# Packed first loads, early squares and pinned conversions in a two-layer decoder step

## The chip, the core and the metric

The kernel runs on one core of one Trainium2 chip. The metric is the device time of one launch in microseconds, the median of several runs. The profile is of one execution; its rows count from the start of the span.

## The reference

Two layers of a decoder are run for a prompt of 256 rows and eight single-row samples (together T = 264 columns) with shared weights, all in float32. Cut to the part around the change:

```python
def moba_gmlp_mixer(x, pos, past_kv, norm_g, w_in, sgu_gain, sgu_w, sgu_b, w_out):
    h = rmsnorm(x, norm_g)
    z = h @ w_in                                  # 1024 -> q, k, v, bu, bv of 512 each
    q, k = rope_partial(q), rope_partial(k)
    a = moba_attention(q, k_all, v_all, pos)      # prompt: causal softmax; samples: 256 paged rows and their own
    bvn = layer_norm(gelu(bv), sgu_gain)
    b_out = spatial_gating(gelu(bu), bvn, sgu_w, sgu_b)
    return x + concat([a, b_out]) @ w_out
```

A convolutional feed-forward network follows, then a second layer (stick-breaking attention, pooling), another such network and a last RMSNorm. All projections, k and v of both layers and some states are outputs.

## The kernel before, in words

X is held transposed, 128 features by 264 columns in eight slices, the weights as 1472 blocks of 128x128 in the order of use. To keep float32 accuracy every operand is split in a high part of type fp32r and the rest: a block costs three matmuls (lines 329 high by high, 330 weight high by operand rest, 331 weight rest by operand high) that add up in a PSUM bank. The high part of eight blocks (a "tile", `wh`) is made by an ACT copy of 128x1024 (line 306), the rest (`wl`) by a DVE subtraction (line 307); `split` looks three tiles ahead, and there are four buffers of each. Raw weights come in chunks, the first six of 8 blocks (512 KB), then of 16 (1 MB), into a ring of three buffers (`rawp`), by DMAs that SP issues. The text numbers chunks (raw0 to raw5 hold blocks 0 to 47, raw6 holds 48 to 63, raw7 64 to 79), tiles (wh0, wh1, ..., eight blocks each) and blocks (0 to 159 are layer 0's input projection, 160 to 223 its output projection).

The order of instructions on an engine is the list scheduler's, except where `tc.keep_in_program_order` pins one. `run` walks through the blocks and calls hooks: `hk.at(n, f)` calls f after 8(n+1) blocks. Engines take their instructions strictly in that order.

**Opening.** Four loads of X on ACT's queue (lines 343 to 345), raw0 in three pieces, raw1 and raw2 on SP (346 to 351). Eight matmuls of 512 columns on a constant (355 to 357) run before the first operand is there. The first 32 blocks are the four q outputs: for the first five slices of X in turn all four outputs, then the rest output by output (`q0`). For each slice `operand_tile` makes the high part on ACT (373) and the rest on DVE (374), and `Norm.add` squares it on ACT (386) and adds on POOL (395, 398). Two matmuls (406) sum over the partitions; Ln and Exp (408, 409) make R, the reciprocal norm; `rope` is R times cosines and sines on DVE (609 to 611). `in0_evac` takes a finished output from PSUM: for q and k a shuffle (635), two multiplications (637 or 639 on DVE, 640 on POOL) and an addition (641). There are four PSUM banks for projections (`psm`) and four for everything else (`at`). SP reads the sixteen page numbers of the samples into registers (424), each when its first page is loaded; K and V pages are loaded in drips of two.

**Attention and gate.** `s_qk` starts a score bank with a matmul of the mask (658), two heads at a time; ACT makes the exponentials and the normalisation (671 to 675), PE the transposes (684). `masks` converts constants to bf16 on DVE (618 to 624). The gate: gelu of bv at hook GM = 12 (759), the sum for the mean on DVE and that for the variance on POOL (751 to 753), `gm_norm`, transposes, four small matmuls (786), an addition on DVE (787), a multiplication on POOL (790), and `halves` (413, 414) for the operand `catB` with which the output projection begins.

Of the kernel before, what the change touches and what calls it, by code (L numbers as in the profile page):

```python
# [9 lines left out]
F32 = mybir.dt.float32  # L10
# [8 lines left out]
P = 128  # L19
# [18 lines left out]
KQ = 5  # L38
PINM = 8
SQL = 2  # L40
XD = (1, 2, 4, 8)
WARM = 8
YD = ((0, 1), (1, 3), (3, 5), (5, 7), (7, 8))
# [3 lines left out]
GG = 16  # L47
GM = 12
GV = 13.5
# [10 lines left out]
MSK = 4.5  # L60
KL = 0
VL = 9
# [60 lines left out]
def _pack_weights(w_in0, w_out0, w_in1, w_out1, gate, up, down):  # L123
# [28 lines left out]
    return np.concatenate(out)  # L152

# [17 lines left out]
def _consts():  # L171
# [36 lines left out]
_INS = [  # L208
    ("w", (_NB * P * P,)), ("x", (P, KD + KD * T)), ("vec", (P, _NVEC)), ("cst", _CST_ARR.shape), ("rope", (P, 2 * T)),
    ("kt0", (NPHYS, P, 512)), ("vp0", (NPHYS, P, 512)), ("kt1", (NPHYS, P, 512)), ("vp1", (NPHYS, P, 512)),  # L210
# [11 lines left out]
def tile_decoder_step(ctx: ExitStack, tc: tile.TileContext, a):  # L222
# [23 lines left out]

    XG = con.tile([P, KD + KD * T], F32, name="XG")
    GAIN = XG[:, :KD]
    X = XG[:, KD:].rearrange("p (m t) -> p m t", t=T)
    VEC = con.tile([P, _NVEC], F32, name="VEC")  # L250
# [22 lines left out]
    raws, splits = {}, {}  # L273

    def raw(ci):
        if ci not in raws:
            n = _CHUNKS[ci] * P
            r = rawp.tile([P, n], F32, tag="raw", name=f"raw{ci}")
            o = coff[ci] * P * P
            src = a["w"][o:o + P * n].rearrange("(p f) -> p f", p=P)  # L280
            raws[ci] = r
            if ci == 0:
                return lambda c, e: nc.sync.dma_start(r[:, c * P:e * P], src[:, c * P:e * P])
            nc.sync.dma_start(r, src)
        return raws[ci]
# [4 lines left out]
    def split(t):  # L290
        for tt in range(len(splits), min(t + (LOOK if pos[0] else 0), NT - 1) + 1):
# [5 lines left out]
            h = wsp.tile([P, 8 * P], F32R, tag="wh", name=f"wh{tt}")  # L297
            l = wsp.tile([P, 8 * P], F32R, tag="wl", name=f"wl{tt}")
            splits[tt] = (h, l)
            if tt == 0:  # L300
                def piece(c, e, h=h, l=l, src=src):
                    c, e = c * P, e * P
                    tc.keep_in_program_order(v.tensor_copy(h[:, c:e], src[:, c:e]))
                    tc.keep_in_program_order(v.tensor_tensor(l[:, c:e], src[:, c:e], h[:, c:e].bitcast(F32), ALU.subtract))
                return piece
            s.activation(h, src, AF.Copy)  # L306
            v.tensor_tensor(l, src, h.bitcast(F32), ALU.subtract)  # L307
        return splits[t]

    def run(order, rhs, evac, hooks=None):  # L310
        hooks = sorted((hooks or {}).items())
        n = 0
        seen, left, ps = {}, {}, {}
        for m, k in order:
            left[m] = left.get(m, 0) + 1
        for m, k in order:
            i = pos[0]
            pos[0] += 1
            h, l = split(i // 8)
            c = (i % 8) * P  # L320
            if m not in ps:
                ps[m] = psm.tile([P, 512], F32, tag="mm", name=f"mm{i}")
# [6 lines left out]
            pe.matmul(o, h[:, c:c + P], xh, start=first, stop=False)  # L329
            pe.matmul(o, h[:, c:c + P], xl, start=False, stop=False)  # L330
            pe.matmul(o, l[:, c:c + P], xh, start=False, stop=left[m] == 0)  # L331
# [7 lines left out]
    orders = dict(_PHASES)  # L339


    CS = f4("ropecs", (P, 2, T))
    xcut = [0] + [KD + e * T for e in XD]
    for b, e in zip(xcut, xcut[1:]):
        nc.scalar.dma_start(XG[:, b:e], a["x"][:, b:e])
    part = raw(0)
    part(0, 2)
    part(2, 4)
    part(4, 8)
    raw(1)  # L350
    raw(2)
    s.preload_act_table_set("natural_log_exp_and_others")
    warm = con.tile([P, 512], BF16, name="warm")
    v.memset(warm, 1.0)
    pw = at("warm")
    for i in range(WARM):
        tc.keep_in_program_order(pe.matmul(pw, warm[:, :P], warm, start=i == 0, stop=i == WARM - 1))

    def late(dst, src):
        tc.keep_in_program_order(nc.sync.dma_start(dst, src))  # L360

# [17 lines left out]
    class Norm:  # L379
# [3 lines left out]

        def add(self, m, pin=False):
            q = sm.tile([P, T], F32, tag="sq", name=f"sq_{self.name}{m}")
            i = s.activation(q, X[:, m, :], AF.Square)
            if pin:
                tc.keep_in_program_order(i)
# [10 lines left out]

        def finish(self):  # L400
            return rstd_of([self.acc] + self.last, 1.0 / D, self.name)

    def rstd_of(parts, scale, name):
        p = at(f"ns_{name}")
        for i, x in enumerate(parts):
            pe.matmul(p[:, :T], ones, x, start=i == 0, stop=i == len(parts) - 1)
        R = sm.tile([P, T], F32, tag="R", name=f"R_{name}", bufs=2)
# [7 lines left out]

    regs = []

    def page_list(cache, name):
# [3 lines left out]
        def load(i):  # L422
            if len(regs) <= i:
                regs.append(nc.sync.value_load(PT[0:1, i:i + 1], min_val=0, max_val=NPHYS - 1))
            if i % NPG == 0:
# [162 lines left out]
    nrm = Norm("n0", True)  # L588
    piece = split(0)
    pieces = [(0, 2), (2, 4), (4, 8)]  # L590
    for m in range(KD):
        if pieces:
            piece(*pieces.pop(0))
        operand_tile(xg[m // 4], m, X[:, m, :], GAIN[:, m:m + 1], pin=m < PINM)
        if m >= SQL:
            nrm.add(m - SQL, pin=m < PINM)
    for m in range(KD - SQL, KD):
        nrm.add(m)
    raw(3)
    late(CS, a["rope"].rearrange("p (c t) -> p c t", c=2))  # L600
    split(1)
    raw(4)
    late(VEC, a["vec"])
    late(PT, a["pt"])
    late(CST, a["cst"])
    R = nrm.finish()

    rope = f4("rope")
    v.tensor_tensor(rope[:, 0, :], CS[:, 0, :], R, ALU.mult)
    v.scalar_tensor_tensor(rope[:, 2, :], CS[:, 1, :], SCALE, R, ALU.mult, ALU.mult)  # L610
    v.tensor_tensor(rope[:, 1, :], CS[:, 1, :], R, ALU.mult)

# [4 lines left out]
    def masks():  # L617
        tc.keep_in_program_order(v.tensor_copy(maskb0[:, 0:P], cst("m0")))
        v.tensor_copy(maskb0[:, SEQ:384], cst("m0"))
        v.tensor_copy(maskb1[:, 0:P], cst("m1"))  # L620
        v.tensor_copy(maskb1[:, SEQ:384], cst("m1"))
        for mk in (maskb0, maskb1):
            g.memset(mk[:, P:SEQ], 0.0)
        v.tensor_copy(identb, ident)

# [4 lines left out]
    def in0_evac(m, o):  # L630
        n, t = m
        if n in "qk":
            d = (q4 if n == "q" else k4)[:, t, :]
# [8 lines left out]
        else:  # L642
            v.tensor_tensor({"v": v4, "bv": bv4, "bu": bu4}[n][:, t, :], o, R, ALU.mult)

# [96 lines left out]
    def sgu_load():  # L741
        late(sguc[:, 0], a["sguw"].rearrange("p (g t) -> p g t", t=P))
        late(sguc[:, 1], a["sgub"].rearrange("p (g t) -> p g t", t=P))
        tril = sm.tile([P, P], F32, tag="tril", name="tril", bufs=1)
        v.tensor_scalar(tril, cst("m0"), 0.0, None, ALU.is_lt)
        v.tensor_tensor(tril, tril, ident, ALU.add)
# [120 lines left out]
    negU = con.tile([P, P], F32R, name="negU")  # L867
    v.tensor_copy(negU, cst("negU"))
    nonesr = con.tile([P, P], F32R, name="nonesr")
# [156 lines left out]
def _lay(inp):  # L1026
# [6 lines left out]
            "cw": col(f["ffn_conv_w"].reshape(-1)), "cb": col(f["ffn_conv_b"].reshape(-1)),  # L1033
            "w00": np.tile(f["l0_sgu_w"][:, 0, 0][None, :], (P, 1)), "b00": np.tile(f["l0_sgu_b"][:, 0][None, :], (P, 1))}
    return {
        "w": _pack_weights(f["l0_w_in"], f["l0_w_out"], f["l1_w_in"], f["l1_w_out"], f["ffn_w_gate"], f["ffn_w_up"], f["ffn_w_down"]),
        "x": np.concatenate([col(f["l0_norm"]), x.T.reshape(KD, P, T).transpose(1, 0, 2).reshape(P, KD * T)], 1),
        "vec": np.concatenate([vecs[n] for n in _VEC], 1),
# [50 lines left out]
```

## Time and profile before

| what | value |
|---|---|
| time, median of 3 runs | 618.89 us (617.85 to 619.99) |
| the profiled execution's own time | 618.47 us |
| its span | 616.4 us |
| mean granted TensorE clock | 0.996 |
| PE busy | 599.4 us, 4924 matmuls |
| moved by DMA | 121.40 MB, mean 197 GB/s |

The profiled execution takes 2.07 us more than its span. A PE row lasts longer than the distance to the next one, since matmuls overlap, so gaps are read from starts. In a row of the chain or the timeline the first number is the start, the second the duration. A row with SPq or ACTq is an issue of that engine's queue and not the transfer.

### The profile page before, as it was taken

The page shows a single profiled execution, that of the slowest core. Times are in us where ns is not written, and L with a number is a line of the kernel's source. Part 1 is how long each engine was busy: PE and PEld are TensorE (multiplying, and loading weights), DVE is VectorE, ACT ScalarE, POOL GpSimd, SP SyncE. Part 2 cuts the span into 40 slices and gives each one's busy share as a digit, 9 for nine tenths or more (in the row PEclk, how much of TensorE's full clock was granted, in tenths as well). Part 3 has the DMA queues.
Part 4 walks back from the last instruction along what each step waited for, and adds up shares of the span by engine and source line. Part 5 has one row for each costly group of instructions (what it writes and reads, how often), then busy time and mean ns, then how long its engine had stood idle before and what let it go on. Part 6 is the DMA issues. An engine that isn't in the chain of part 4 may idle for free.

```text
span 616.4 us, 12351 instructions
## 1 busy us (share of the span) xinstructions
PE 599.4 (97%) x4924; PEld 575.3 (93%) x4924; DVE 413.1 (67%) x704; ACT 350.4 (57%) x621; POOL 84.9 (14%) x111
## 2 busy tenths in 40 slices
PE   7899999999999999999999999999999999999994
PEld 5788987999999999999999997899999999999994
DVE  6986663969976676655555686396996766764441
ACT  5459763767756555644442757376765555554441
POOL 3330132324200000001110000042420000001020
PEclk9999999999999999999999999999999999999998
DMA  7995873543655445695477559944364555554502
GB/s 259 325 403 220 328 258 54 206 153 133 216 184 205 158 184 205 228 392 200 155 229 262 219 184 141 134 175 172 136 215 170 200 182 167 199 189 166 200 1 70
DMA packets 41354, 121.40 MB, mean 197 GB/s; under 512 B 17490, under 2 KB 19410, under 8 KB 29906
## 3 DMA queue, kind: packets, MB, share of 16 engines
q1 hardware_dynamic: 40178, 119.00, 59.3%
q10 hardware_dynamic: 1120, 1.63, 0.9%
q8 instruction: 38, 0.62, 0.4%
q14 instruction: 18, 0.15, 0.1%
HBM read 116.67 MB, written 3.94 MB: 196 GB/s over the span
## 4 chain that ended last, share of the span: by engine, by line
PE 84%; DVE 7%; issue 3%; DMA 2%; ACT 2%; POOL 1%; SPq 0%; DVEq 0%; ACTq 0%
PE mm L330 26%; PE mm L329 25%; PE mm L331 25%; DMA raw<-in_w 2%; DVE wl L307 2%; DVE xn_l L374 1%; PE pv_l L465 1%; PE sc L451 1%; PE pav L494 1%; PE Z L900 1%; DVE wk L542 1%; ACT wh L306 1%; PE Z L884 1%; POOL wk L553 0%; PE pt L684 0%
## 5 line engine op out<-in xcount | busy, mean ns | idle before, releaser
L307 DVE TENSOR_TENSOR wl<-raw,wh 128x1024 fp32r<-128x1024 f32 x183 | 229.4, 1255 | 129.1 <-ACT wh L306 129.0
L306 ACT ACTIVATE wh<-raw 128x1024 fp32r<-128x1024 f32 x183 | 193.7, 1059 | 182.5 <-PE mm L330 169.3
L330 PE MATMUL mm<-xn_l,wh 128*128 128x264 f32 x544 | 154.7, 284 | 1.7 <-DVE xn_l L374 1.5
L329 PE MATMUL mm<-xn_h,wh 128*128 128x264 f32 x544 | 153.8, 283 | 0.0
L331 PE MATMUL mm<-xn_h,wl 128*128 128x264 f32 x544 | 153.4, 283 | 0.0
L330 PEld LDWEIGHTS mm<-xn_l,wh 128*128 128x128 f32 x544 | 102.3, 188 | 2.5 <-DVE xn_l L374 2.5
L329 PEld LDWEIGHTS mm<-xn_h,wh 128*128 128x128 f32 x544 | 102.1, 188 | 0.0
L331 PEld LDWEIGHTS mm<-xn_h,wl 128*128 128x128 f32 x544 | 102.1, 188 | 0.0
L330 PE MATMUL mm<-a_l,wh 128*128 128x264 f32 x352 | 99.8, 284 | 0.0
L329 PE MATMUL mm<-a_h,wh 128*128 128x264 f32 x352 | 99.5, 284 | 0.0
L331 PE MATMUL mm<-a_h,wl 128*128 128x264 f32 x352 | 99.4, 283 | 0.0
L331 PEld LDWEIGHTS mm<-a_h,wl 128*128 128x128 f32 x352 | 66.2, 188 | 0.0
L330 PEld LDWEIGHTS mm<-a_l,wh 128*128 128x128 f32 x352 | 66.2, 188 | 0.0
L329 PEld LDWEIGHTS mm<-a_h,wh 128*128 128x128 f32 x352 | 66.0, 188 | 0.0
L329 PE MATMUL mm<-xg_h,wh 128*128 128x264 f32 x160 | 46.6, 298 | 3.6 <-DVE q L637 1.6
L330 PE MATMUL mm<-xg_l,wh 128*128 128x264 f32 x160 | 46.1, 293 | 0.0
L331 PE MATMUL mm<-xg_h,wl 128*128 128x264 f32 x160 | 44.7, 291 | 1.3 <-DVE wl L307 1.3
L329 PE MATMUL mm<-xg_f_h,wh 128*128 128x264 f32 x160 | 45.8, 286 | 0.0
L330 PE MATMUL mm<-xg_f_l,wh 128*128 128x264 f32 x160 | 45.4, 284 | 0.0
L331 PE MATMUL mm<-xg_f_h,wl 128*128 128x264 f32 x160 | 45.3, 283 | 0.0
L329 PE MATMUL mm<-xg_n_h,wh 128*128 128x264 f32 x128 | 37.4, 292 | 0.0
L331 PE MATMUL mm<-xg_n_h,wl 128*128 128x264 f32 x128 | 36.8, 288 | 0.0
(266 smaller groups left out, 1074.5 us busy)
## 6 DMA issues: line engine op xcount, KB each, us to landing
raw<-in_w SPq DMA_DIRECT2D x89, 1024.0 KB, 4.8
K<-in_kt SPq DMA_DIRECT2D x32, 256.0 KB, 6.0
V<-in_vp SPq DMA_DIRECT2D x32, 256.0 KB, 5.6
raw<-in_w SPq DMA_DIRECT2D x5, 512.0 KB, 5.3
CST<-in_cst SPq DMA_DIRECT2D x1, 548.0 KB, 5.5
XG<-in_x ACTq DMA_DIRECT2D x1, 528.0 KB, 7.8
out_k<-k SPq DMA_DIRECT2D x1, 528.0 KB, 9.4
out_v<-v SPq DMA_DIRECT2D x1, 528.0 KB, 3.0
```

Source lines behind the costliest of these rows:

```text
L306: s.activation(h, src, AF.Copy)
L307: v.tensor_tensor(l, src, h.bitcast(F32), ALU.subtract)
L329: pe.matmul(o, h[:, c:c + P], xh, start=first, stop=False)
L330: pe.matmul(o, h[:, c:c + P], xl, start=False, stop=False)
L331: pe.matmul(o, l[:, c:c + P], xh, start=False, stop=left[m] == 0)
L374: j = v.scalar_tensor_tensor(l, src, gain, h.bitcast(F32), ALU.mult, ALU.subtract)
L451: pe.matmul(ps[32 * t:32 * t + 32, :PAST].rearrange("p (g k) -> p g k", g=NPG), qz[:, t, sq, :], kt[sq][:, :, t * P:(t + 1) * P], start=sq ...
L465: pe.matmul(pv[32 * j:32 * j + 32, :], pz[:, pg, sq, :], vtiles[sq][:, pg, :], start=pg == 0, stop=pg == NPG - 1)
L494: pe.matmul(o, vt[:, 0, h * HD:(h + 1) * HD], w[:, :SEQ], start=True, stop=False)
L542: v.scalar_tensor_tensor(C[:, 1:SEQ], G[:, 0:SEQ - 1], wc(1, j), C[:, 1:SEQ], ALU.mult, ALU.add)
L884: tc.keep_in_program_order(pe.matmul(ps[:, 0:SEQ], kh[:, 0:P], qh[:, 0:SEQ], start=False, stop=False, skip_group_check=True))
L900: pe.matmul(ps[:, 0:384], negU, x, start=False, stop=False, skip_group_check=True)
```

## The change

- The first sixteen blocks, the gain and all of X come in six loads, each a contiguous pack of the blocks and the slices that are used together (`_FIRST`): gain, blocks 0-1, slice 0; blocks 2-3, slice 1; blocks 4-7, slice 2; blocks 8-11, slice 3; blocks 12-15, slice 4; slices 5 to 7. Packs 1 and 3 go on ACT's queue, the others on SP's. raw2 to raw5 get buffers of the pool `up` and not of the ring of three, so they are issued without a wait for a buffer.
- The page table is loaded third on ACT's queue, and the sixteen register reads stand on SP between the loads of raw3 to VEC, which are now pinned.
- Blocks 2 to 15 get their high part on ACT and not on DVE; squares are taken from the packs, and pinned between; tiles 2, 3 and 4 are pinned there too.
- `norm0` (R and rope) is a hook at 3.25, after block 33. Finished outputs wait in a list until then, and the outputs that start at blocks 32 and 40 get a bank of `at` (`spare`).
- X itself is loaded in four parts at hooks 14 to 17, for the residual: 1 MB more.
- Conversions of constants are pinned, the gelu of bv too, at hook 11 and not 12; the variance's sum goes to DVE; K's drip starts at hook 1 and not 0; the opening's constant matmuls are 12 of 256 columns and not 8 of 512.

```diff
-PINM = 8
-SQL = 2
-XD = (1, 2, 4, 8)
-WARM = 8
+WARM = 12
-GM = 12
+GM = 11
-KL = 0
+KL = 1
+_FIRST = [((0, 2), (0, 1)), ((2, 4), (1, 2)), ((4, 8), (2, 3)), ((8, 12), (3, 4)), ((12, 16), (4, 5)), ((0, 0), (5, 8))]
...
+            r = f4(f"raw{ci}", (P, n)) if ci < C8 else rawp.tile([P, n], F32, tag="raw", name=f"raw{ci}")
...
+    spare = (32, 40)
...
+                ps[m] = at(f"mm{i}") if i in spare else psm.tile([P, 512], F32, tag="mm", name=f"mm{i}")
...
+    for i in range(len(_FIRST)):
+        g_, w_, x_ = _first_cols(i)
+        n = g_ + w_ + x_
+        r = f4(f"xw{i}", (P, n))
+        tc.keep_in_program_order((s if i in (1, 3) else nc.sync).dma_start(r, a["xw"][o:o + P * n].rearrange("(p f) -> p f", p=P)))
...
+        if i == 4:
+            raw(2)
+    tc.keep_in_program_order(s.dma_start(PT, a["pt"]))
+    for c in (3, 4):
+        raw(c)
+        page_regs(2)
+    late(CS, a["rope"].rearrange("p (c t) -> p c t", c=2))
+    raw(5)
+    page_regs(4)
+    late(CST, a["cst"])
+    raw(6)
+    page_regs(4)
+    late(VEC, a["vec"])
+    page_regs(4)
...
+    low = part(0, v)
+    operand_tile(xg[0], 0, xin[0], GAIN[:, 0:1], pin=True)
+    low()
+    for m in range(1, 5):
+        part(m, s)()
+        operand_tile(xg[m // 4], m, xin[m], GAIN[:, m:m + 1], pin=True)
+        if m != 2:
+            nrm.add((m - 1) // 2 if m < 4 else 2, xin[(m - 1) // 2 if m < 4 else 2])
+    whole(2)
+    for m in range(5, KD):
+        operand_tile(xg[m // 4], m, xin[m], GAIN[:, m:m + 1], pin=True)
+    for m in range(3, KD):
+        nrm.add(m, xin[m])
+        if m == 4:
+            whole(3)
+        elif m == 6:
+            whole(4)
...
-    SUM1, SUM2 = v, g
+    SUM1, SUM2 = v, v
...
-        s.activation(bv4, bv4, AF.Gelu_apprx_tanh)
+        tc.keep_in_program_order(s.activation(bv4, bv4, AF.Gelu_apprx_tanh))
...
+    hk.at(3.25, norm0)
+    for m in range(0, KD, 2):
+        hk.at(14 + m / 2, lambda m=m: late(X[:, m:m + 2, :], a["x"].rearrange("p (m t) -> p m t", t=T)[:, m:m + 2, :]))
```

`part` converts the blocks of one pack, `whole` a tile of eight blocks from its chunk, both as `split` does, pinned; `page_regs(n)` reads the next n page numbers.

More of the change, by code (lines that the diff above doesn't have):

```diff
@@ L151, in _pack_weights, with _first_cols, _pack_first @@
         o += c
-    return np.concatenate(out)
+    return out
+_FIRST = [((0, 2), (0, 1)), ((2, 4), (1, 2)), ((4, 8), (2, 3)), ((8, 12), (3, 4)), ((12, 16), (4, 5)), ((0, 0), (5, 8))]
+def _first_cols(i):
+    (b, e), (m, n) = _FIRST[i]
+    return (KD if i == 0 else 0), (e - b) * P, (n - m) * T
+def _pack_first(gain, x, chunks):
+    w = np.concatenate([c.reshape(P, -1) for c in chunks[:2]], 1)
+    rows = []
+    for i, ((b, e), (m, n)) in enumerate(_FIRST):
+        rows.append(np.concatenate(([gain] if i == 0 else []) + [w[:, b * P:e * P], x[:, m:n].reshape(P, -1)], 1).reshape(-1))
+    return np.concatenate(rows)
 _VEC = {}
@@ L208 @@
 _INS = [
-    ("w", (_NB * P * P,)), ("x", (P, KD + KD * T)), ("vec", (P, _NVEC)), ("cst", _CST_ARR.shape), ("rope", (P, 2 * T)),
+    ("w", ((_NB - 16) * P * P,)), ("xw", (P * (KD + 16 * P + KD * T),)), ("x", (P, KD * T)), ("vec", (P, _NVEC)), ("cst", _CST_ARR.shape), ("rope", (P, 2 * T)),
     ("kt0", (NPHYS, P, 512)), ("vp0", (NPHYS, P, 512)), ("kt1", (NPHYS, P, 512)), ("vp1", (NPHYS, P, 512)),
@@ L273, in tile_decoder_step, with late, wtiles @@
     raws, splits = {}, {}
+    def late(dst, src):
+        tc.keep_in_program_order(nc.sync.dma_start(dst, src))
+    def wtiles(tt):
+        return [wsp.tile([P, 8 * P], F32R, tag=f"w{x}", name=f"w{x}{tt}") for x in "hl"]
     def raw(ci):
@@ L277, in raw @@
             n = _CHUNKS[ci] * P
-            r = rawp.tile([P, n], F32, tag="raw", name=f"raw{ci}")
-            o = coff[ci] * P * P
-            src = a["w"][o:o + P * n].rearrange("(p f) -> p f", p=P)
+            r = f4(f"raw{ci}", (P, n)) if ci < C8 else rawp.tile([P, n], F32, tag="raw", name=f"raw{ci}")
+            o = (coff[ci] - 16) * P * P
             raws[ci] = r
-            if ci == 0:
-                return lambda c, e: nc.sync.dma_start(r[:, c * P:e * P], src[:, c * P:e * P])
-            nc.sync.dma_start(r, src)
+            late(r, a["w"][o:o + P * n].rearrange("(p f) -> p f", p=P))
         return raws[ci]
@@ L290, in split @@
     def split(t):
-        for tt in range(len(splits), min(t + (LOOK if pos[0] else 0), NT - 1) + 1):
+        for tt in range(len(splits), min(t + LOOK, NT - 1) + 1):
             ci = chunk_of[tt]
@@ L296, in split @@
             src = raws[ci][:, o:o + 8 * P]
[L297 to L305, printed above, removed]
+            h, l = splits[tt] = wtiles(tt)
             s.activation(h, src, AF.Copy)
@@ L339, in tile_decoder_step, with page_regs @@
     orders = dict(_PHASES)
+    regs = []
+    def page_regs(n):
+        for i in range(len(regs), len(regs) + n):
+            regs.append(nc.sync.value_load(PT[0:1, i:i + 1], min_val=0, max_val=NPHYS - 1))
     CS = f4("ropecs", (P, 2, T))
[L343 to L354, printed above, removed]
+    first, o = [], 0
+    for i in range(len(_FIRST)):
[3 more added lines that the diff above has]
+        tc.keep_in_program_order((s if i in (1, 3) else nc.sync).dma_start(r, a["xw"][o:o + P * n].rearrange("(p f) -> p f", p=P)))
+        o += P * n
+        first.append((r[:, :g_], r[:, g_:g_ + w_], r[:, g_ + w_:].rearrange("p (m t) -> p m t", t=T)))
+        if i == 4:
[12 more added lines that the diff above has]
+    page_regs(4)
+    GAIN = first[0][0]
+    xin = [x[:, i, :] for _, _, x in first for i in range(x.shape[1])]
+    tc.keep_in_program_order(s.preload_act_table_set("natural_log_exp_and_others"))
+    warm = con.tile([P, 256], BF16, name="warm")
+    tc.keep_in_program_order(v.memset(warm, 1.0))
     pw = at("warm")
     for i in range(WARM):
-        tc.keep_in_program_order(pe.matmul(pw, warm[:, :P], warm, start=i == 0, stop=i == WARM - 1))
-    def late(dst, src):
-        tc.keep_in_program_order(nc.sync.dma_start(dst, src))
+        tc.keep_in_program_order(pe.matmul(pw[:, :256], warm[:, :P], warm, start=i == 0, stop=i == WARM - 1))
     ident = cst("ident")
@@ L382, in __init__, with add @@
             self.acc = None
-        def add(self, m, pin=False):
+        def add(self, m, src=None):
             q = sm.tile([P, T], F32, tag="sq", name=f"sq_{self.name}{m}")
-            i = s.activation(q, X[:, m, :], AF.Square)
-            if pin:
+            i = s.activation(q, X[:, m, :] if src is None else src, AF.Square)
+            if src is not None:
                 tc.keep_in_program_order(i)
@@ L398, in add, with finish, rstd_of @@
                 g.tensor_tensor(self.acc, self.acc, q, ALU.add)
-        def finish(self):
-            return rstd_of([self.acc] + self.last, 1.0 / D, self.name)
-    def rstd_of(parts, scale, name):
+        def finish(self, pin=False):
+            return rstd_of([self.acc] + self.last, 1.0 / D, self.name, pin)
+    def rstd_of(parts, scale, name, pin=False):
         p = at(f"ns_{name}")
         for i, x in enumerate(parts):
-            pe.matmul(p[:, :T], ones, x, start=i == 0, stop=i == len(parts) - 1)
+            mm = pe.matmul(p[:, :T], ones, x, start=i == 0, stop=i == len(parts) - 1)
+            if pin:
+                tc.keep_in_program_order(mm)
         R = sm.tile([P, T], F32, tag="R", name=f"R_{name}", bufs=2)
@@ L588, in tile_decoder_step @@
     nrm = Norm("n0", True)
[L589 to L604, printed above, removed]
@@ L605, in tile_decoder_step, with part @@
-    late(CST, a["cst"])
-    R = nrm.finish()
-    rope = f4("rope")
-    v.tensor_tensor(rope[:, 0, :], CS[:, 0, :], R, ALU.mult)
-    v.scalar_tensor_tensor(rope[:, 2, :], CS[:, 1, :], SCALE, R, ALU.mult, ALU.mult)
-    v.tensor_tensor(rope[:, 1, :], CS[:, 1, :], R, ALU.mult)
+    for tt in range(2):
+        splits[tt] = wtiles(tt)
+    def part(i, eng):
+        (b, e), _ = _FIRST[i]
+        h, l = [w[:, (b % 8) * P:(b % 8) * P + (e - b) * P] for w in splits[b // 8]]
+        src = first[i][1]
+        tc.keep_in_program_order(s.activation(h, src, AF.Copy) if eng is s else v.tensor_copy(h, src))
+        return lambda: tc.keep_in_program_order(v.tensor_tensor(l, src, h.bitcast(F32), ALU.subtract))
@@ new lines, in whole @@
+    def whole(tt):
+        h, l = splits[tt] = wtiles(tt)
+        ci = chunk_of[tt]
+        o = (tt * 8 - coff[ci]) * P
+        src = raws[ci][:, o:o + 8 * P]
+        tc.keep_in_program_order(s.activation(h, src, AF.Copy))
+        tc.keep_in_program_order(v.tensor_tensor(l, src, h.bitcast(F32), ALU.subtract))
+    low = part(0, v)
[6 more added lines that the diff above has]
+            nrm.add((m - 1) // 2 if m < 4 else 2, xin[(m - 1) // 2 if m < 4 else 2])
@@ new lines, in tile_decoder_step, with norm0 @@
+    whole(2)
[7 more added lines that the diff above has]
+            whole(4)
+    rope = f4("rope")
+    R0, held = [], []
+    def norm0():
+        R = nrm.finish(pin=True)
+        R0.append(R)
+        v.tensor_tensor(rope[:, 0, :], CS[:, 0, :], R, ALU.mult)
+        v.scalar_tensor_tensor(rope[:, 2, :], CS[:, 1, :], SCALE, R, ALU.mult, ALU.mult)
+        v.tensor_tensor(rope[:, 1, :], CS[:, 1, :], R, ALU.mult)
+        for m, o in held:
+            in0_evac(m, o)
@@ L618, in masks @@
         tc.keep_in_program_order(v.tensor_copy(maskb0[:, 0:P], cst("m0")))
-        v.tensor_copy(maskb0[:, SEQ:384], cst("m0"))
-        v.tensor_copy(maskb1[:, 0:P], cst("m1"))
-        v.tensor_copy(maskb1[:, SEQ:384], cst("m1"))
+        tc.keep_in_program_order(v.tensor_copy(maskb0[:, SEQ:384], cst("m0")))
+        tc.keep_in_program_order(v.tensor_copy(maskb1[:, 0:P], cst("m1")))
+        tc.keep_in_program_order(v.tensor_copy(maskb1[:, SEQ:384], cst("m1")))
         for mk in (maskb0, maskb1):
             g.memset(mk[:, P:SEQ], 0.0)
-        v.tensor_copy(identb, ident)
+        tc.keep_in_program_order(v.tensor_copy(identb, ident))
     q4, k4, v4 = f4("q4"), f4("k4"), f4("v4")
@@ L631, in in0_evac @@
         n, t = m
+        if not R0:
+            held.append((m, o))
+            return
         if n in "qk":
@@ L642, in in0_evac @@
         else:
-            v.tensor_tensor({"v": v4, "bv": bv4, "bu": bu4}[n][:, t, :], o, R, ALU.mult)
+            v.tensor_tensor({"v": v4, "bv": bv4, "bu": bu4}[n][:, t, :], o, R0[0], ALU.mult)
     ktiles, kload = page_list(a["kt0"], "K0")
@@ L744, in sgu_load @@
         tril = sm.tile([P, P], F32, tag="tril", name="tril", bufs=1)
[L745 removed]
+        tc.keep_in_program_order(v.tensor_scalar(tril, cst("m0"), 0.0, None, ALU.is_lt))
         v.tensor_tensor(tril, tril, ident, ALU.add)
@@ L867, in tile_decoder_step @@
     negU = con.tile([P, P], F32R, name="negU")
-    v.tensor_copy(negU, cst("negU"))
+    tc.keep_in_program_order(v.tensor_copy(negU, cst("negU")))
     nonesr = con.tile([P, P], F32R, name="nonesr")
@@ L1034, in _lay @@
             "w00": np.tile(f["l0_sgu_w"][:, 0, 0][None, :], (P, 1)), "b00": np.tile(f["l0_sgu_b"][:, 0][None, :], (P, 1))}
+    ws = _pack_weights(f["l0_w_in"], f["l0_w_out"], f["l1_w_in"], f["l1_w_out"], f["ffn_w_gate"], f["ffn_w_up"], f["ffn_w_down"])
+    xt = x.T.reshape(KD, P, T).transpose(1, 0, 2)
     return {
-        "w": _pack_weights(f["l0_w_in"], f["l0_w_out"], f["l1_w_in"], f["l1_w_out"], f["ffn_w_gate"], f["ffn_w_up"], f["ffn_w_down"]),
-        "x": np.concatenate([col(f["l0_norm"]), x.T.reshape(KD, P, T).transpose(1, 0, 2).reshape(P, KD * T)], 1),
+        "w": np.concatenate(ws[2:]),
+        "xw": _pack_first(col(f["l0_norm"]), xt, ws),
+        "x": xt.reshape(P, KD * T),
         "vec": np.concatenate([vecs[n] for n in _VEC], 1),
```

8 lines of the change are left out of this document (1 added, 7 removed).

## The prediction

> **What bounds the kernel now.** The page comes first (parts 1 and 4), then PE's waits over the whole span.
>
> ```profile
> PE 599.4 (97%) x4924; PEld 575.3 (93%) x4924; DVE 413.1 (67%) x704; ACT 350.4 (57%) x621; POOL 84.9 (14%) x111
> PE 84%; DVE 7%; issue 3%; DMA 2%; ACT 2%; POOL 1%; SPq 0%; DVEq 0%; ACTq 0%
> ```
> ```profile
> PE mm L329 <- DVE q L637: 1.6, 1, 1.6
> PE mm L329 <- ACT wh L306: 1.3, 1, 1.3
> PE mm L331 <- DVE wl L307: 1.3, 1, 1.3
> PE mm L329 <- ACT catB_h L413: 0.7, 1, 0.7
> PE mm L329 <- DVE wh L303: 0.6, 1, 0.6
> ```
>
> PE is the bound: 97% busy, 84% of the chain. A change that adds or removes no projection block can only fill PE's holes, and the named waits are few and small. The opening has more than they say. The timeline gives the distance between main matmuls when nothing is missing, and then the opening itself:
>
> ```profile
> 62.15 0.28 PE L329 MATMUL mm<-xg_h,wh 128*128 128x264 f32 x1
> 62.51 0.28 PE L329 MATMUL mm<-xg_h,wh 128*128 128x264 f32 x1
> ```
> ```profile
> 4.51 0.98 PE L329 MATMUL mm<-xg_h,wh 128*128 128x264 f32 x2
> ...
> 6.55 0.42 PE L330 MATMUL mm<-xg_l,wh 128*128 128x264 f32 x1
> 6.77 0.42 PE L329 MATMUL mm<-xg_h,wh 128*128 128x264 f32 x1
> ...
> 8.41 0.29 PE L330 MATMUL mm<-xg_l,wh 128*128 128x264 f32 x1
> 8.53 0.28 PE L329 MATMUL mm<-xg_h,wh 128*128 128x264 f32 x1
> ...
> 19.36 0.61 PE L406 MATMUL ns_n<-acc_n,ones 128*128 128x264 f32 x2
> ...
> 24.92 0.36 PE L329 MATMUL mm<-xg_h,wh 128*128 128x264 f32 x1 [1.60 <-DVE q L637]
> ...
> 30.82 0.28 PE L329 MATMUL mm<-xg_h,wh 128*128 128x264 f32 x1
> ```
>
> From 62.15 to 62.51 three matmuls pass, so a block takes about 0.3645 us (0.1215 a matmul). The row at 24.92 starts block 32, the one at 30.82 block 48. 48 blocks are 17.50 us; from 4.51 to 30.82 there are 26.31. So 8.8 us are lost before block 48, nearly all before block 32 (32 blocks are 11.66, and 20.41 passed). Parts of it: the first matmuls are 0.22 apart (6.55, 6.77) and later 0.12 (8.41, 8.53), about 1.1 us in all; five of the waits above, 5.5 with catB's, of which catB's 0.7 lies elsewhere; the sums for the norm, 0.5; the rest are small gaps.
>
> What feeds PE then, by windows (columns: stretch, length, busy time of PE, PEld, DVE, ACT, POOL, granted clock, DMA share, GB/s):
>
> ```profile
> 0.00:4.50 4.50, 3.04 (x8) 1.05 (x9) 1.39 (x7) 1.80 (x2) 1.16 (x8) 1.00 0.52 145
> 4.50:25.00 20.50, 15.59 (x103) 14.08 (x102) 17.59 (x34) 11.84 (x23) 6.89 (x8) 1.00 0.89 296
> 25.00:42.00 17.00, 16.73 (x137) 15.86 (x138) 16.37 (x38) 6.77 (x10) 6.07 (x9) 1.00 1.03 396
> 42.00:62.00 20.00, 20.00 (x204) 16.91 (x203) 12.42 (x36) 19.48 (x56) 1.27 (x1) 1.00 0.69 262
> 62.00:87.00 25.00, 25.00 (x207) 24.86 (x205) 15.70 (x24) 17.60 (x27) 4.19 (x7) 1.00 0.80 285
> ```
>
> The reader is to see a bound that changes hands under a PE that looks full: up to 25 DVE and the loads, from 25 to 42 DVE (16.37 of 17.00), from 42 to 62 ACT with the softmax (19.48 of 20.00). PE gets ahead in the first stretch only as far as DVE and ACT let the attention follow.
>
> **The change part by part.** *Loads.* The bytes stay: X and the first sixteen blocks are 2.1 MB either way, in packs of 260 to 396 KB. No row shows such a size; the neighbours do (KB, us to landing):
>
> ```profile
> raw<-in_w SPq DMA_DIRECT2D x5, 512.0 KB, 5.3
> XG<-in_x ACTq DMA_DIRECT2D x1, 136.0 KB, 3.1
> raw<-in_w SPq DMA_DIRECT2D x2, 128.0 KB, 3.4
> ```
>
> A pack takes 3.1 to 5.3 us. For the first two, both needed for block 2, I take 3.5, nearest to the small rows, so they land near 4.3 and the first matmul starts at about 4.85, 0.3 later than now (bounds 0 and +2). Against the consumption of PE the packs stand well: pack 2 near 7.2 serves block 4 (then at 7.5), pack 4 near 8.2 serves block 12 (about 10.7), and raw2 to raw5, issued without a ring's wait, land near 9.6, 11.9, 13.2 and 15.2 for blocks 16, 24, 32 and 40, due at 12.1, 15, 18 and 21. So the waits for wh, wl and the 1.3 us ones go. In the opening remain 1.1 us of wide pitch, 0.5 of sums and 0.6 of gaps, an estimate.
>
> *raw6 and the registers.* Now raw6 stands behind a buffer and one register read:
>
> ```profile
> 17.67 0.48 SPq L424
> ...
> 19.19 5.33 DMA raw<-in_w
> ```
> ```profile
> L424 SPq TENSOR_LOAD <-PT x16: 262/268/482, 17.7 to 40.3; - x16
> ```
>
> It lands at 24.52. After, all sixteen reads are on SP between loads: eight of them ahead of raw6, at about 0.6 us each with their two companions and 0.4 for an issue. Bytes are the other side: up to raw6's end 6.1 MB have to arrive, of which 0.65 come by 4.5 (145 GB/s). The remaining 5.46 MB take 18.4 us at 296 GB/s and 13.8 at 396, so raw6 lands at 22.9 or 18.3. I take 19.4, near the faster row, since these loads are as wide as those between 25 and 42; that is 5 us earlier than now. raw7 goes out near 20, behind eight more reads and two K loads, and lands at 24.9 to 26.5.
>
> *ACT and DVE.* Thirteen of sixteen early blocks move from DVE to ACT; the duration is in these rows (busy us, mean ns):
>
> ```profile
> L306 ACT ACTIVATE wh<-raw 128x1024 fp32r<-128x1024 f32 x5 | 5.3, 1054 | 4.3 <-DMA raw<-in_w 4.3
> L373 ACT ACTIVATE xg_h<-XG 128x264 fp32r<-128x264 f32 x8 | 4.1, 506 | 2.5 <-DMA XG<-in_x 2.3
> L386 ACT ACTIVATE sq_n<-XG 128x264 f32<-128x264 f32 x8 | 3.2, 408 | 0.0
> ```
>
> ACT had 11.84 of 20.50 busy; two tiles of 1.05 more in four pieces (about 2.3) fit in. In the new order R's two ACT instructions stand behind wh6 and wh7, which is an added wait: R waits for raw6. Behind R nothing urgent is queued on ACT, but rope on DVE waits for it, and every q and k evacuation waits for rope. R is ready three to three and a half us behind raw6 (two conversions of 1.05, Ln and Exp, wl7 ahead on DVE). With 19.4 the rope starts at 22.9; it now starts here:
>
> ```profile
> 23.32 0.42 DVE L609 TENSOR_TENSOR rope<-ropecs,R_n 128x264 f32<-128x264 f32 x1
> ```
>
> So PE is much earlier and rope only 0.4 us. The two spare banks let PE run until block 48 without rope (now it stops at block 32 for 1.6). Block 48 thus comes at 4.85 + 17.50 + 2.2 = 24.55, 6.3 us earlier than 30.82, and meets the first evacuation of q there (about 24.4 to 24.9).
>
> *DVE until the first scores.* DVE's chain from rope to the first maximum of the scores is not shorter; the rows of its end:
>
> ```profile
> 40.35 0.41 DVE L669 TENSOR_REDUCE st<-S 128x1 f32<-128x256 f32 x1
> ...
> 40.79 0.37 ACT L671 ACTIVATE p<-S,st 128x128 f32<-128x128 f32 x1 [2.35 <-DVE st L669]
> ...
> 42.47 0.37 ACT L671 ACTIVATE p<-S,st 128x128 f32<-128x128 f32 x1 [0.77 <-DVE st L669]
> ```
> ```profile
> L307 DVE TENSOR_TENSOR wl<-raw,wh 128x1024 fp32r<-128x1024 f32 x8 | 11.4, 1422 | 1.0 <-ACT wh L306 1.0
> ```
>
> Eight subtractions of 1422 ns are 11.4 of its time, and two of them (wl6, wl7) move ahead of rope; in their place come the constants' casts and a wait for raw7 of 0 to 2.5 us (I take 1) ahead of wl8. The softmax then begins at about 40.5 against 40.79. It keeps ACT full for 20 us either way, so PE can't be done with the attention of the prompt more than 0.3 us earlier; but the scheduler has put that attention 31 main matmuls later in PE's order, so when it is done 31 x 0.1215 = 3.8 more work lies behind PE. Of the 6.3 us in hand 3.8 to 4.5 remain at 62. I take 4.5: 0.3 for the earlier start and 0.4 of the 0.77 that ACT waits before the second head pair (42.47).
>
> *End of the input projection.*
>
> ```profile
> 90.57 0.76 PE L329 MATMUL mm<-catB_h,wh 128*128 128x264 f32 x4 [0.66 <-ACT catB_h L413]
> ...
> 91.48 3.64 PE L465 MATMUL pv_l<-V,PZ 128*32 128x512 f32 x32
> ```
>
> In the new order these matmuls of 3.6 us stand ahead of the first block of the output projection, and cover its wait of 0.66 (0.7 with the gap before). The variance's sum, on DVE instead of POOL, and the gelu one hook earlier cost nothing in a stage where DVE has 15.70 of 25.00; without that cover 0.4 us. The extra 1 MB of X at 70 to 85 meets a DMA share of 0.80: hidden; at 285 GB/s it would be 3.7 us of queue if raw were short there.
>
> *Sum.* 4.5 + 0.7 = 5.2 from the profiled 618.47 gives 613.3; that execution lies 0.4 under the median of 618.89, so a median would be 613.3 to 613.7. I say **613.4**.
>
> A rule bears on the 0.22 spacing. The profile's clock column says 1.00 in both first windows, yet the distances 0.22 and 0.12 stand nearly two to one. The Trainium skill, "TensorE: Matmul & The Clock Gate", Part 1, has the array at half clock until a free-running window of about 3.4 us was busy. By that rule it matters that the constant's matmuls end earlier after the change; the price by the rows is rival b.
>
> **The rivals.** *a. Nothing is given back.* DVE's wait for raw7 is 0 and the attention follows: 6.5 + 0.7 = 7.2, 611.3. For it: DVE's 17.59 in the opening loses thirteen casts. Against: 16.37 of 17.00 afterwards.
>
> *b. The slow spacing lasts longer.*
>
> ```profile
> 1.47 3.59 PE L357 MATMUL warm<-warm 128*128 128x512 bf16 x8 [1.47 <-DVE warm L354]
> ...
> 4.49 0.70 PEld L329 LDWEIGHTS mm<-xg_h,wh 128*128 128x128 f32 x2 [0.34 <-ACT xg_h L373]
> ```
>
> The eight constant matmuls of 512 columns become twelve of 256: three quarters of the columns, so 2.7 us, and a smaller constant to fill. They end at about 3.8 to 4.2, and PE then idles up to a microsecond before its first block, against 0.34 now. If the spacing then stays at 0.22 for ten matmuls more, that is 10 x 0.1 = 1.0: 614.3. For it: the spacing changes in the trace only at 7.0, well after the first block. Against: what is lost before block 48 may be hidden by the softmax.
>
> *c. raw7 is late.* The page table, third on ACT's queue, lands late, and the sixteen reads push raw7 by 2.5: DVE stands before wl8 with the evacuations behind it, the softmax starts later by as much: 615.8. For it: now PT's own load isn't on this path.
>
> *d. The gain doesn't pass the softmax.* ACT's 19.48 of 20.00 sets the end of the attention, and the 31 matmuls turn out as waits: only the boundary's 0.7 remains, and some noise: 617.8.
>
> *e. Slower: R behind raw6.* As DVE's chain starts with rope and rope with R, each us that raw6 lands after 19.4 costs one us on the softmax's start and so on PE. At 24.6 (where it lands now) the whole gain is gone, from 26.5 on the kernel is more than 0.3% slower; with 27 to 27.5 it takes 621. For it: eight reads and two waits for completed loads stand ahead of raw6 on SP, and PT's landing ahead of them. Against: both bounds from bytes, 18.3 and 22.9, lie under 24.6.
>
> **How the numbers follow.** Forecast .38, a .20, b .12, c .14, d .09, e .07. About 0.3% (1.9 us) is what a measurement can tell from no change. Faster by more: forecast, a, b, c, .84; within: d, .09; slower: e, .07. The range leaves out d and e: 610.8 (a, with 0.5 to spare) to 616.4 (c, with 0.6).
>
> **What would show it right or wrong.** Right: block 32 near 18.5 and block 48 near 24.6; raw6 landing near 19.4; rope at 22.9; the first exponential of the softmax near 40.5; PE waits of about 2 us in the attention; no wait at the catB boundary, whose first block starts near 85.5. Wrong in a: no waits between 42 and 62. In b: spacing of 0.22 beyond 7.2. In c: DVE idle before wl8. In e: ACT idle before wh6 and rope after 24. The whole is wrong if the stages after 91 don't come out the same, shifted: the sum counts nothing behind that.

## The result, and the profile after

The changed kernel takes 622.73 us (median of 4, 622.02 to 623.91) against 618.64 before: ratio 1.0062, interval 1.0044 to 1.0079. It is slower by 4.1 us; the forecast was 613.4, a gain of 5.2. The span grew from 616.4 to 620.8. First the waits of PE from 25 to 98 (engine and line, what it waited for: us, times, longest), and the windows that were shown of before:

```profile
PE sc L476 <- issue: 2.5, 1, 2.5
PE S L710 <- DVE identb L673: 1.1, 1, 1.1
PE S L712 <- DVE k L693: 0.6, 1, 0.6
PE S L710 <- ACT p L724: 0.5, 1, 0.5
```
```profile
4.50:25.00 20.50, 19.14 (x146) 18.36 (x147) 17.55 (x27) 14.44 (x28) 6.02 (x6) 1.00 0.94 354
25.00:42.00 17.00, 14.41 (x112) 12.71 (x111) 16.06 (x40) 5.19 (x5) 6.96 (x9) 1.00 0.96 383
42.00:62.00 20.00, 17.03 (x141) 15.27 (x143) 13.75 (x40) 17.75 (x50) 1.42 (x1) 1.00 0.83 313
62.00:87.00 25.00, 25.00 (x234) 22.74 (x226) 14.37 (x26) 18.10 (x32) 0.00 (x0) 0.93 0.61 210
```

The opening did what it should: PE does 146 matmuls up to 25 and not 103. What is gained is gone by 62: of the 37 us from 25 to 62 PE has been empty for 5.6. From 62 to 87 PE counts as full, but its clock is 0.93. PE's timeline gives the first block, blocks 32 and 48, and the largest hole:

```profile
5.06 0.82 PE L338 MATMUL mm<-xg_h,wh 128*128 128x264 f32 x4 [1.12 <-ACT xg_h L400]
...
18.59 0.28 PE L338 MATMUL mm<-xg_h,wh 128*128 128x264 f32 x1
...
25.89 0.36 PE L338 MATMUL mm<-xg_h,wh 128*128 128x264 f32 x1 [0.44 <-DVE q L689]
...
61.67 5.35 PE L476 MATMUL sc<-K,qz_l 128*32 128x256 f32 x64 [2.46 <-issue]
```

Block 48 comes at 25.89, 4.9 us earlier than in before. Then PE waits 2.46 us ahead of the sample scores, and their 64 matmuls take 5.35 us; in before they took this:

```profile
56.69 3.66 PE L451 MATMUL sc<-K,qz_l 128*32 128x256 f32 x64
```

"Issue" says that the profile knows no releaser, so we look at what else ends there. ACT's timeline of after from 56, and then that of before around its own gelu:

```profile
56.29 1.28 ACT L811 ACT_TABLE_LOAD   x1
57.58 1.09 ACT L811 ACTIVATE bv<-bv 128x1056 f32<-128x1056 f32 x1
58.58 0.39 ACT L726 ACTIVATE p<-p,st 128x128 f32<-128x128 f32 x1
58.87 0.49 ACT L727 ACTIVATE p<-p,st 128x256 f32<-128x256 f32 x1
59.37 1.28 ACT L723 ACT_TABLE_LOAD   x1
60.66 0.37 ACT L723 ACTIVATE p<-S,st 128x128 f32<-128x128 f32 x1
60.93 0.19 ACT L723 ACTIVATION_READ_ACCUMULATOR p<-S,st 128x1 f32 x1
61.02 0.47 ACT L724 ACTIVATE p<-S,st 128x256 f32<-128x256 f32 x1
61.38 0.20 ACT L724 ACTIVATION_READ_ACCUMULATOR p<-S,st 128x1 f32 x1
```
```profile
55.91 0.50 ACT L672 ACTIVATE p<-S,st 128x256 f32<-128x256 f32 x1
56.26 0.24 ACT L672 ACTIVATION_READ_ACCUMULATOR p<-S,st 128x1 f32 x1
...
58.53 1.28 ACT L759 ACT_TABLE_LOAD   x1
59.82 1.08 ACT L759 ACTIVATE bv<-bv 128x1056 f32<-128x1056 f32 x1
```

The gelu of bv stands ahead of the exponentials of heads 6 and 7, and not behind them as in before: a table load, the gelu, a table load back, 3.65 us on the engine that sets the pace of this stage. PE starts 0.1 us after head 6's second half has been read. The link is a PSUM bank: the four banks of `at` went last to the scores of heads 6 and 7 and to the transposes of heads 4 and 5, so, if they are taken in turn, the sample scores get the bank of head 6. Then the clock:

```profile
60.00:61.60 1.60, 0.00 (x0) 0.00 (x0) 0.00 (x0) 1.59 (x6) 0.00 (x0) 1.00 1.07 448
...
62.50:66.00 3.50, 3.50 (x43) 2.23 (x36) 1.39 (x2) 2.95 (x8) 0.00 (x0) 0.51 0.73 240
66.00:68.00 2.00, 2.00 (x35) 1.29 (x28) 0.00 (x0) 0.46 (x2) 0.00 (x0) 1.00 0.73 252
```

The stretch before 61.6 is empty, and a microsecond later PE runs for 3.5 us at 0.51. The Trainium skill, "TensorE: Matmul & The Clock Gate", Part 1, has the clock fall to one half after an idle window of about 3.4 us; here 2.5 us were enough. Run 2 suggests that they are not in every execution.

The other half is the start of the softmax. ACT's and DVE's timelines show raw6's landing (the wait at 20.92 ends), rope, raw7's landing and the first exponential:

```profile
20.92 2.01 ACT L313 ACTIVATE wh<-raw 128x1024 fp32r<-128x1024 f32 x2 [4.45 <-DMA raw<-in_w]
...
26.81 2.01 ACT L313 ACTIVATE wh<-raw 128x1024 fp32r<-128x1024 f32 x2 [3.06 <-DMA raw<-in_w]
...
42.90 0.37 ACT L723 ACTIVATE p<-S,st 128x128 f32<-128x128 f32 x1 [4.95 <-DVE st L721]
```
```profile
24.29 0.43 DVE L656 TENSOR_TENSOR rope<-ropecs,R_n 128x264 f32<-128x264 f32 x1
```

The softmax starts 2.1 us later than in before, though PE is 4.9 us ahead.

### The profile page after: what moved, and what is told of

Read it like the earlier page. It is cut to its first block, busy times and chain, and to the rows that moved or that the text cites. A ratio compares the mean times of both kernels' runs of the same rounds, so it can differ in the third digit from the quotient of the medians.

```text
span 620.8 us, 12357 instructions
## 1 busy us (share of the span) xinstructions
PE 602.0 (97%) x4928; PEld 577.8 (93%) x4928; DVE 414.3 (67%) x706; ACT 350.0 (56%) x624; POOL 82.2 (13%) x108
## 4 chain that ended last, share of the span: by engine, by line
PE 69%; DVE 5%; issue 1%; ACT 0%; POOL 0%; DVEq 0%; ACTq 0%
PE mm L339 22%; PE mm L338 22%; PE mm L340 21%; DVE xn_l L401 1%; DVE wl L314 1%; PE Z L955 1%; PE pv_l L490 1%; PE sc L476 1%; DVE wk L567 1%; PE Z L939 1%; DVE wk L563 0%; DVE wk L568 0%; PE pav L519 0%; DVE wk L577 0%; DVE X L1077 0%
## 5 line engine op out<-in xcount | busy, mean ns | idle before, releaser
L314 DVE TENSOR_TENSOR wl<-raw,wh 128x1024 fp32r<-128x1024 f32 x179 | 222.6, 1245 | 127.2 <-ACT wh L313 127.1
L313 ACT ACTIVATE wh<-raw 128x1024 fp32r<-128x1024 f32 x179 | 189.3, 1059 | 178.5 <-PE mm L339 160.2
L339 PE MATMUL mm<-xg_l,wh 128*128 128x264 f32 x160 | 44.4, 289 | 0.3 <-DVE xg_l L401 0.3
L340 PE MATMUL mm<-xg_h,wl 128*128 128x264 f32 x160 | 43.3, 286 | 0.3 <-DVE wl L631 0.3
```

## The experiments

Theory A: ACT's two table loads among the exponentials cost PE a wait and then its clock. B: the sample scores wait for the K pages, which go out later now. C: all is due to the late softmax. The first four runs shared their runs of before (618.76).

**1. The gelu late.**

```diff
-GM = 11
+GM = 13
```

> After with GM = 13 and not 11; the order on PE, DVE and SP is unchanged, and on ACT the gelu of bv with its table load stands behind the last exponentials of the softmax and not ahead of those of heads 6 and 7. Theory A (ACT reloads a table ahead of those exponentials, PE waits for the bank they read, idles 2.5 us and does the 64 sample score matmuls at half clock): the wait at the sample scores goes, the 64 take 3.7 and not 5.35 us, total about 4.3 less, 618.4. Rival B (the sample scores wait for the K pages, whose drip starts a hook later and whose last two go out at 45): no change, 622.7. Rival C (the whole loss is the softmax that starts 2.1 us later than before): no change, 622.7.

Measured: 618.72, ratio to before 0.9998 (0.9987 to 1.0008), 4.0 less than after. The wait is gone and the scores take 3.66 us again:

```profile
58.59 3.66 PE L476 MATMUL sc<-K,qz_l 128*32 128x256 f32 x64
```

A is borne out: 2.46 and 1.69 (5.35 less 3.66) are 4.15. B falls, as nothing of the K pages was touched. C is not all. (The order on DVE is not quite unchanged: two reciprocals of the softmax and one subtraction change places.)

**2. raw6 and raw7 early.**

```diff
     raw(5)
+    raw(6)
     page_regs(4)
     late(CST, a["cst"])
-    raw(6)
+    raw(7)
...
-        hk.at(KL + n, drip_of(kload, 2))
+        hk.at(3 + n, drip_of(kload, 3))
```

> After with raw6 and raw7 ahead of the constants and of eight and twelve register reads on SP, and the K pages from hook 3 in threes; nothing moves on PE, ACT and DVE. Theory A: rope, and with it the softmax, starts 1.5 to 2.5 us earlier (raw6 near 19.4 and not 20.9, raw7 near 24 and not 26.8); the gelu keeps its place, and the stall stays; total 1.5 to 2.5 less, about 620.8. Rival B: the K pages come later still, so the sample scores wait longer: 622.7 or slower. Rival C: all of the loss goes with the start of the softmax, 618.5.

Measured: 618.54, ratio 0.9991 (0.9978 to 1.0004). The first exponential comes 3.3 us earlier, more than A had named, and so is the gain, 4.2; 0.7 of it lies behind block 224 (runs 8 to 10).

```profile
21.93 0.43 DVE L657 TENSOR_TENSOR rope<-ropecs,R_n 128x264 f32<-128x264 f32 x1
```
```profile
39.60 0.37 ACT L724 ACTIVATE p<-S,st 128x128 f32<-128x128 f32 x1 [4.09 <-DVE st L722]
```

The hole is as it was:

```profile
58.39 5.35 PE L477 MATMUL sc<-K,qz_l 128*32 128x256 f32 x64 [2.46 <-issue]
```

The time alone is C's; the row keeps A apart, since the hole stands unchanged and merely comes earlier. B falls again: the K pages go out later still.

The twelve executions of this run fall into two groups. In seven the span is 616.4 to 616.9 us and the mean granted clock 0.993 or 0.994; in five the span is 615.0 to 615.4 and the clock 0.995 or 0.996. The profile is of the first group, and its one stretch at half clock in the middle of the kernel (59.5 to 63.0) accounts for the difference in the mean: 3.4 us at one half are 0.003 of the span. So the same hole seems to bring the clock down in some executions only, and the fall costs about 1.6 us where it comes. For the five this is inferred from their clock, as they left no trace.

**3. Both.** The two edits together.

> After with both edits, GM = 13 and the earlier raw6 and raw7. Theory A: both gains, about 6.3, 616.4, so faster than before by 2. Rival B: 622.7 or slower. If what is left after that is over 3 us above the 613.4 that was forecast, a third cause is open (the slower pace of the later stages, 1.5 us in the trace, is a candidate).

Measured: 615.0, ratio 0.9937 (0.9922 to 0.9952), faster than before. From 42 to 62 PE is full again, ahead of an ACT that is full too:

```profile
42.00:62.00 20.00, 19.97 (x203) 16.64 (x202) 12.75 (x34) 19.94 (x56) 0.09 (x1) 1.00 0.94 348
```

Singly the edits take off 4.0 and 4.2, together 7.7; by the median spans (620.7 in after, 612.55 here) 8.1. The two costs add up, nearly. Block 224, the first of the feed-forward network, comes 5.1 us earlier than in before (122.04, shown below):

```profile
116.90 0.28 PE L338 MATMUL mm<-xg_f_h,wh 128*128 128x264 f32 x1
```

**4. The two table loads put into before.** The result of the small gelu is overwritten. The scheduler answered by more than the two loads: on ACT one copy of transposed probabilities now stands between them, and seven main matmuls on PE and one instruction on DVE changed places.

```diff
         pr = pp.tile([P, 384], F32, tag="p", name=f"p0_{h}")
+        if h == 6:
+            s.activation(pr[:, 0:1], st[:, 0:1], AF.Gelu_apprx_tanh)
```

> Before with one gelu of 128x1 ahead of the exponentials of head 6, whose result is overwritten: two table loads of 1.28 us and 0.2 more on ACT in the middle of the softmax, and nothing else. Theory A: PE waits at the sample scores or the transposes behind them and loses 2 to 4.5 us (the upper value if the clock falls as well): 620.5 to 623. Rival B and C: ACT's delay is absorbed, 618.6 to 619.

Measured: 622.75, ratio 1.0066 (1.0049 to 1.0082): 4.0 us for 2.8 us on ACT. PE waits elsewhere this time, at the transposes and the samples' probabilities, and the clock falls behind it as well. This execution also had half clock twice in the opening, at 12.5 and 26.2, where the profile of before had none: it is 0.9 us late by block 96, and the other 3.6 us of its delay at block 224 come behind the inserted gelu. The windows stand for one stretch at half clock, 70.55 to 73.97:

```profile
PE pP L722 <- DVE psamp L713: 1.1, 1, 1.1
...
PE pt L686 <- ACT pT L687: 0.5, 1, 0.5
```
```profile
70.00:72.00 2.00, 2.00 (x13) 2.00 (x13) 0.72 (x2) 1.06 (x1) 0.00 (x0) 0.64 1.05 402
72.00:75.00 3.00, 3.00 (x18) 2.83 (x17) 1.25 (x2) 0.39 (x1) 0.00 (x0) 0.67 0.44 102
```

**5 and 6. Which load?** Both with GM = 13: in run 5 the K pages from hook 3 as above and the rest as in after; in run 6 raw6 ahead of CST and four reads, K as in after.

> The gelu late (GM = 13) and, on SP alone, the K pages behind raw7 and raw8 (from hook 3 in threes); CST and VEC and all register reads stay ahead of raw7. To be compared with the run of GM = 13 alone (618.7). If raw7, for which the DVE waits ahead of wl8, is what starts the softmax late: raw7 lands 1.5 to 2.5 us earlier, the softmax starts near 40.5 and not 42.3, 617.2. If raw6 with R behind it is: no change, 618.7.

> The gelu late (GM = 13) and, on SP alone, raw6 ahead of CST and of the four register reads in front of it; K stays ahead of raw7. To be compared with GM = 13 alone (618.7). If raw6 with R behind it starts the softmax late: rope 1.5 to 2 us earlier (near 22.7), the softmax as much, 617.0. If raw7 is the step: rope earlier, DVE then waits longer ahead of wl8, softmax near 42, 618.7.

Measured (before 618.63): 616.65 for run 5, ratio 0.9965 (0.9952 to 0.9978), and 618.07 for run 6, 0.9988 (0.9979 to 0.9997). In run 6 rope stands at 21.81, but the gain stops at raw7, and PE waits for the constants that stand behind its subtraction on DVE:

```profile
26.97 2.01 ACT L313 ACTIVATE wh<-raw 128x1024 fp32r<-128x1024 f32 x2 [5.72 <-DMA raw<-in_w]
...
43.09 0.37 ACT L723 ACTIVATE p<-S,st 128x128 f32<-128x128 f32 x1 [3.80 <-DVE st L721]
```
```profile
PE S L710 <- DVE identb L673: 2.1, 1, 2.1
```

So raw7 seems to be the greater part (2.1 us against 0.7), and only both give 3.7: two links of one chain. Two reservations. 0.66 of the 2.1 and of the 3.7 is not the softmax but the pace after block 224, which is 485.65 in run 5 and 486.30 in run 1; and the 0.7 of run 6 is hardly clear of noise, as its interval overlaps that of run 1. Neither profile shows an early softmax: that of run 5 is of its slowest execution (618.15), with raw6 at 22.6, and in that of run 6 the first exponential comes later than in run 1 (42.34). What is said of the two runs rests on the times.

**7. PE kept busy until its first block.** `WARM = 18` on top of run 3.

> The run with both edits (615.0) with 18 constant matmuls and not 12, so that PE works until its first block. If PE's idle stretch of 1.3 us ahead of the first block keeps the wide spacing (0.22) on, it ends by 7 in every execution, and the median falls by 0.5 to 1.0, 614.3. If the end of the wide spacing has its own phase (it came at 5.3, 7.2 and 8.8 in three executions): 615.0.

Measured: 614.44 (614.20 to 614.52), ratio 0.9927 (0.9914 to 0.9941); 0.56 less than run 3, but not by the spans, whose medians are 612.5 and 612.55. Windows of the same 4.8 us, run 3 and then run 7:

```profile
4.80:9.60 4.80, 4.77 (x24) 4.77 (x25) 4.43 (x9) 4.59 (x12) 1.03 (x1) 1.00 1.03 414
```
```profile
4.80:9.60 4.80, 4.62 (x36) 4.39 (x36) 4.34 (x9) 4.50 (x12) 1.02 (x1) 1.00 1.03 417
```

24 matmuls against 36, and the clock column says 1.00 to both. The trace's own list of clock changes begins only with the change to full clock, at 8.76 in run 3 and at 4.36 in run 7, there where the spacing narrows; the column counts what lies ahead of the first entry as full. Yet block 32 starts at 18.32 in run 7 and 18.35 in run 3, and block 224 at 117.05 and 116.90: nothing is left of it. Run 8, with 12 constant matmuls, takes 614.56, so the 0.56 is not a gain of the constant matmuls. Runs 7 to 9 are level, some 4 us below before.

**8 to 10. The slower pace of the later stages.** From block 224 to block 1471 PE and ACT have the same instructions in the same order as in before, and DVE too but for the place of one cast; X lies in another buffer. All the same (before, then after):

```profile
122.04 0.28 PE L329 MATMUL mm<-xg_f_h,wh 128*128 128x264 f32 x1
...
606.83 0.28 PE L329 MATMUL mm<-a_h,wh 128*128 128x264 f32 x1
```
```profile
124.73 0.28 PE L338 MATMUL mm<-xg_f_h,wh 128*128 128x264 f32 x1
...
611.04 0.28 PE L338 MATMUL mm<-a_h,wh 128*128 128x264 f32 x1
```

484.8 us in before and in run 4, 486.3 in after, runs 1 and 6, 485.6 in runs 2, 3, 5, 7 and 8: a property of the kernel and not of the execution, as far as one profile of each tells. The groups are those of the K pages: 486.3 with K in twos from hook 1, 485.6 in threes from hook 3. Run 8 took 14 unused buffers, run 9 held one through the first feed-forward network, run 10 is before with the K pages from hook 3:

> The run with both edits (615.0) with 14 more buffers taken, and not used, from the pool of 24 ahead of the first feed-forward network. After has ten more tiles in this pool ahead of that place than before, so 14 more make the same turn of the ring. If the place of the operands makes the slower pace after block 224 (484.8 us in before, 485.6 in the run with both edits, 486.3 in after): 484.8, 614.2 in all. If not: 485.6, 615.0.

> The run with both edits and 18 constant matmuls (614.4), with one more buffer of the pool of 24 written ahead of the first feed-forward network and read (a copy of 128x264 on POOL) behind it, so that it is held through it; the order on PE, ACT and DVE is the same. If the pace after block 224 hangs on the buffers that the operands get: blocks 224 to 1471 take another time than 485.63, by 0.2 or more either way, and the total moves as much. If not: 485.6 and 614.4.

> Before with the K pages from hook 3 in threes; the order on PE, ACT and DVE is the same, on SP the K pages stand behind raw7. If the pace after block 224 hangs on the order in which the pages take buffers: blocks 224 to 1471 take another time than 484.8. If the loads ahead of raw7 delayed the softmax in before too (it starts at 40.8): the softmax up to 1 us earlier, 618; otherwise 618.7.

Measured: run 8 614.56, stretch 485.6, no change. Run 9 614.51 and 485.5; its parts moved both ways (blocks 224 to 752 by +0.2, 768 to 1264 by -0.35), its sum by less than the 0.2 named. Run 10 619.29, ratio 1.0015 (1.0006 to 1.0024), with the stretch at 486.0:

```profile
121.56 0.28 PE L329 MATMUL mm<-xg_f_h,wh 128*128 128x264 f32 x1
...
607.56 0.29 PE L329 MATMUL mm<-a_h,wh 128*128 128x264 f32 x1
```

In before the same edit of the K pages makes the stretch 1.2 us longer, in after 0.7 us shorter, some 60 us and more after the last of these pages has been used, and with the same order of instructions on PE, ACT and DVE. (The whole of run 10 loses 0.6 only, since block 224 comes 0.5 earlier.) That the buffers' places do it is the nearest explanation, and not shown: runs 8 and 9, which moved buffers, changed the stretch by 0.12 at most.

## Why the prediction was wrong

- **The step that failed first** is "the gelu one hook earlier cost nothing". It was priced as work in a stage where DVE has room; it is ACT's instruction, and its place on ACT among the exponentials was not looked up. The premise "it keeps ACT full for 20 us either way" took the softmax's ACT time as fixed; two table loads and the gelu came into it. They are 3.65 us of ACT; PE waited 2.46 us for them and then ran 3.4 us at half clock. Cost: 4.0 us by run 1; run 4, which puts two table loads into before, has 4.0 too. None of it stood in any rival.
- **The loads of raw6 and raw7** were mis-sized. The mechanism was on record as rivals c and e. raw6 landed at 20.9 and not 19.4, rope came at 24.29 and not 22.9, raw7 at 26.8, and the softmax at 42.90 and not 40.5. Together 3.7 to 4.2 us (runs 2 and 3), of which 0.7 is the pace after block 224. The bounds from bytes were right for the sum (raw6 within 18.3 to 22.9), but they were not carried on to the softmax, and the price of c, 2.5, was held to be unlikely.
- **The opening** was right in kind: block 32 at 18.59 (said: near 18.5), block 48 at 25.89 (24.6), 4.9 of the 6.3 us. The first block is 0.2 later than said, and behind it 3.3 us are lost up to block 48, where the sum had 2.2; 0.6 of these 1.1 is block 48's wait for q (from 24.93 to 25.89, less one block), late with rope, and the rest is open. One term of it was misread: six blocks, 2 to 7, move from DVE to ACT, and not thirteen or fourteen, since in before ACT makes the high part of blocks 8 to 15 already (an ACT copy of 128x1024 at 10.13). The six fitted in: from 4.5 to 25 ACT's busy time went from 11.84 to 14.44 us. DVE's stayed (17.59 and 17.55), though rival a counted on thirteen casts less.
- **The sheer position** ("31 main matmuls later in PE's order") worked once the two costs were gone: in run 3 block 224 comes 5.1 us earlier than in before, where the sum said 5.2. That they agree so well is partly luck: the softmax started at 39.30 and not 40.5, and the boundary gave less than was counted.
- **The boundary** gave little. The wait for catB is gone, but 0.4 for catA's rest is new (at 107.65, and in run 3 too), so about 0.3 of the 0.7 remains. The sign "first block near 85.5" left out the 3.64 us of matmuls that now stand ahead of it; with them it is near 89, and run 3 has 89.49.
- **Rival b** was right about the spacing (0.22 up to 8.8 in run 3, up to 4.4 in run 7), but its price of 1.0 us is not seen: the spans of runs 3 and 7 are level. Against it the prediction had named that such a loss may be hidden. (Rival a counts 6.5 where the text has 6.3 in hand; no row gives the 0.2.)
- **That the stages after 91 come out the same** is wrong by 1.5 us in after and 0.85 in run 3. The order of the K pages is part of it; why is open.

From 613.4 to 622.7 it is 4.0 for the gelu, 3.7 for the loads and the 1.6 by which run 3 lies above the forecast. This 1.6 is a remainder: 0.85 of it is the later pace, 0.2 the end of the kernel, 0.1 was missing at block 224, and the rest, about half a microsecond, lies between executions and outside the span.

## What to carry to other kernels

When an activation moves, look for its place on ACT among activations of another table: two loads of 1.28 us were more than the function (1.09), and where ACT sets a stage's pace they reach PE, with the clock on top in some executions. When an opening is made faster, follow the next chunk of weights to the instruction that stands behind its conversion; what is queued there, and not PE, decides what is kept of the gain.

## What the runs showed of the hardware

- A hole of 2.46 us in PE (after and run 2) and one of 2.12 us (run 6, at 31.26) were followed, 0.9 to 1.4 us after work had begun again, by half clock (in after 0.43 against 0.22 us for four score matmuls): 1.7 us on top of the hole. In five of run 2's twelve executions the mean clock says that the fall did not come.
- Each stretch at half clock between two stretches at full clock in these traces, one each in after, run 2 and run 6 and three in run 4, is 3.41 us long.
- With 12 constant matmuls, the last of which starts 1.2 to 1.5 us ahead of the first block, the spacing of 0.22 lasted until 8.3 to 9.8 in six profiles (the seventh, that of after, has the narrow spacing from 5.3); with 18 it ended at 4.4 and 4.6 (runs 7 and 9). Whether the gap or the smaller number of constant matmuls keeps it is not separated. The clock column shows 1.00 throughout, as it has no entry ahead of the first change.
- The pace of the same 1247 blocks differs by up to 1.5 us between kernels with the same order of matmuls there, and repeats within 0.14 us inside each of the groups named under runs 8 to 10.
